# Down products as seven of quadrants, and weight sums made by transfers in memory, in a two-layer block kernel

## The chip, the cores and the metric

The kernel runs on one core of a Trainium2 chip. A core has a matrix engine (TensorE, PE in the profile; its weight loads are shown apart as PEld), a vector engine (VectorE, DVE), a scalar engine (ScalarE, ACT), GpSimd (POOL), and SyncE (SP), which here only issues transfers. Each engine works through its own queue in order and waits on semaphores of the others. Transfers run on 16 DMA engines that all queues share. The metric is the time of one execution on the device in microseconds (us), as the median of several runs.

## The reference

Two layers over 512 tokens of width 1024, all in f32. Layer 0 mixes tokens by a gated unit with a causal matrix per chunk of 128, layer 1 by forgetting attention with 12 heads; both add 4 heads of attention over 256 memory rows. After each mixing comes a gated feed-forward of hidden width 2816, which is what the change touches:

```
h = h + rmsnorm(mixed @ w_out[layer], ln_mix_post[layer])
f = rmsnorm(h, ln_ffn_pre[layer])
f = (silu(f @ w_ffn_gate[layer]) * (f @ w_ffn_up[layer])) @ w_ffn_down[layer]
h = h + rmsnorm(f, ln_ffn_post[layer])
```

## The kernel before

Every f32 number goes into TensorE as a pair of parts, hi (rounded) and lo (the rest), and a product is three matmuls, hi x hi, hi x lo and lo x hi (`mm3`, lines 182 to 184). ScalarE makes hi by a cast and VectorE lo by a subtraction (`split`, lines 239 and 240); eight buffers each of 128 x 512 hold split weights (`pair_of_parts`). A weight piece is loaded as a raw tile of 128 x 1024 (512 KB) by SP into one of four buffers.

The hidden width is 22 tiles of 128. Tiles 0 and 1 of gate and up are computed plainly while the mixing of the layer before ends (`boundary`), and their down product gives the first value of `ys`, the eight accumulators of 128 tokens x 512 outputs. The other 20 tiles go in pairs. For a pair of tiles, gate and up are each an instance of `Seven` (from line 999): the 256 rows of output, 512 tokens and 1024 inputs are cut into quadrants, and seven products of quadrants take the place of eight. `combined` makes the seven forms of the inputs once per layer. The forms of the weights need four sums, made on VectorE from two raw tiles (`sums`, lines 1022 to 1027, s3, a21 + a22, and two more), and each of the seven forms is split. `run` does one product (12 matmuls of 256 columns into a PSUM tile a, e or x) and ScalarE copies what is to be kept; `end` has VectorE add up the two halves (lines 1060, 1061, 1063) and hands them to `gate_rows` or `up_rows`, which scale, apply silu or multiply, and split the product into `fs`. `sevens` (line 1066) orders the seven products: 1, 7, 2, 6, 4, 3, 5.

`feed_forward` (line 1089) has the pairs in groups of 6, 6, 4 and 4 tiles. After each group but the last come its down products: for each half of the outputs, four PSUM tiles of 128 x 512 take 3 matmuls of 512 columns for each tile of hidden width, and VectorE adds each to `ys` (line 1174). `down_weights` loads two tiles of hidden width for one half of the outputs and splits two pieces. The last group's down products are part of `tail_of`, which also finishes the norm and, in the boundary that follows, the turn back to rows of features.

The order on each engine is set when the program is built, by a scheduler that plans the instructions with costs of its own; `behind` and `issue_after` hold an instruction back behind a named one. `last_sum` names the two sums after which the down weights may be split. A tile's buffer is given again when all its readers are done, so a load of SP waits for the split (lines 239 and 240) that read the buffer last.

## Time and profile before

| what | us |
|---|---|
| runs, median (lowest to highest) | 1113.89 (1113.71 to 1114.05) |
| profiled execution, span from first to last instruction | 1111.4 |
| TensorE busy | 1100.8 (99%) |
| VectorE busy | 893.7 (80%) |
| ScalarE busy | 660.5 (59%) |
| GpSimd busy | 25.3 (2%) |
| loads, q1 | 116.18 MB, 33.4% of 16 engines |

The profile shows one execution; its span is 2.5 us shorter than the median of the runs, which is what lies around the first and last instruction. Busy times are shares of that span. Matmuls overlap, so a record of 0.39 us can follow the one before by 0.23; the same holds to a smaller degree on VectorE and ScalarE, so costs are taken from starts, not from records. The feed-forward of layer 0 runs from about 192 to 515 us, that of layer 1 from about 778 to the end. The wait printed in square brackets is the idle time of the engine before the instruction and what ended it.

### The profile page before, as it was taken

The page shows a single profiled execution, that of the slowest core. Times are in us where ns is not written, and L with a number is a line of the kernel's source. Part 1 is how long each engine was busy: PE and PEld are TensorE (multiplying, and loading weights), DVE is VectorE, ACT ScalarE, POOL GpSimd, SP SyncE. Part 2 cuts the span into 40 slices and gives each one's busy share as a digit, 9 for nine tenths or more (in the row PEclk, how much of TensorE's full clock was granted, in tenths as well). Part 3 has the DMA queues.
Part 4 walks back from the last instruction along what each step waited for, and adds up shares of the span by engine and source line. Part 5 has one row for each costly group of instructions (what it writes and reads, how often), then busy time and mean ns, then how long its engine had stood idle before and what let it go on. Part 6 is the DMA issues. An engine that isn't in the chain of part 4 may idle for free.

```text
span 1111.4 us, 19500 instructions
## 1 busy us (share of the span) xinstructions
PE 1100.8 (99%) x7382; PEld 1000.1 (90%) x7382; DVE 893.7 (80%) x1735; ACT 660.5 (59%) x1397; POOL 25.3 (2%) x42
## 2 busy tenths in 40 slices
PE   9999999999999999999999999999999999999997
PEld 7998889998899898998988898889999899899996
DVE  8889658997697597896987898858997697687875
ACT  8776468664365264577665667668665265254553
POOL 0100000000000000001000000000000000000000
PEclk9999999999999999999999999999999999999999
DMA  7522322334133323343322654422224133333222
GB/s 267 162 76 77 98 74 76 115 109 141 57 112 97 117 92 114 97 148 117 104 88 62 173 132 116 131 76 74 79 90 154 62 114 96 101 109 114 77 76 76
DMA packets 64421, 118.12 MB, mean 106 GB/s; under 512 B 5260, under 2 KB 40088, under 8 KB 64328
## 3 DMA queue, kind: packets, MB, share of 16 engines
q1 hardware_dynamic: 63720, 116.18, 33.4%
q8 instruction: 58, 0.95, 0.4%
q0 software_dynamic: 192, 0.52, 0.2%
q14 instruction: 35, 0.29, 0.1%
q10 hardware_dynamic: 416, 0.18, 0.1%
HBM read 104.71 MB, written 2.10 MB: 96 GB/s over the span
## 4 chain that ended last, share of the span: by engine, by line
PE 94%; ACT 3%; DVE 1%; issue 1%; POOL 0%; DMA 0%; POOLq 0%; DVEq 0%; ACTq 0%
PE y L182 10%; PE y L183 10%; PE y L184 10%; PE a L182 5%; PE a L184 5%; PE a L183 5%; PE x L184 3%; PE e L182 3%; PE e L184 3%; PE e L183 3%; PE x L183 3%; PE x L182 3%; PE ps L184 3%; PE ps L183 3%; PE ps L182 3%; PE v L182 2%
## 5 line engine op out<-in xcount | busy, mean ns | idle before, releaser
L239 ACT CAST whi<-raw 128x512 fp32r<-128x512 f32 x460 | 273.1, 620 | 217.7 <-PE y L184 89.1
L240 DVE TENSOR_TENSOR wlo<-raw,whi 128x512 fp32r<-128x512 f32 x460 | 303.5, 684 | 69.5 <-ACT whi L239 67.8
L182 PE MATMUL y<-whi,fhi 128*128 128x512 f32 (+1 forms) x356 | 140.2, 394 | 0.4 <-DVE y L838 0.4
L184 PE MATMUL y<-whi,flo 128*128 128x512 f32 (+1 forms) x356 | 139.3, 391 | 0.0
L183 PE MATMUL y<-wlo,fhi 128*128 128x512 f32 (+1 forms) x356 | 139.2, 391 | 0.0
L184 PE MATMUL x<-xshi,wlo 128*128 128x256 f32 x320 | 89.9, 281 | 0.0
L182 PE MATMUL a<-xshi,whi 128*128 128x256 f32 x320 | 89.8, 281 | 0.0
L183 PE MATMUL x<-xslo,whi 128*128 128x256 f32 x320 | 89.7, 280 | 0.0
L182 PE MATMUL x<-xshi,whi 128*128 128x256 f32 x320 | 89.7, 280 | 0.0
L183 PE MATMUL a<-xslo,whi 128*128 128x256 f32 x320 | 89.7, 280 | 0.0
L184 PE MATMUL a<-xshi,wlo 128*128 128x256 f32 x320 | 89.6, 280 | 0.0
L184 PEld LDWEIGHTS y<-whi,flo 128*128 128x128 f32 x356 | 66.8, 188 | 15.7
L182 PEld LDWEIGHTS y<-whi,fhi 128*128 128x128 f32 x356 | 66.8, 188 | 15.6 <-DVE y L838 0.7
L183 PEld LDWEIGHTS y<-wlo,fhi 128*128 128x128 f32 x356 | 66.9, 188 | 14.7
L182 PEld LDWEIGHTS a<-xshi,whi 128*128 128x128 f32 x320 | 60.2, 188 | 0.5
L183 PEld LDWEIGHTS a<-xslo,whi 128*128 128x128 f32 x320 | 60.2, 188 | 0.3
L184 PEld LDWEIGHTS x<-xshi,wlo 128*128 128x128 f32 x320 | 60.3, 188 | 0.0
L183 PEld LDWEIGHTS x<-xslo,whi 128*128 128x128 f32 x320 | 60.2, 188 | 0.0
L184 PEld LDWEIGHTS a<-xshi,wlo 128*128 128x128 f32 x320 | 60.2, 188 | 0.0
L182 PEld LDWEIGHTS x<-xshi,whi 128*128 128x128 f32 x320 | 60.2, 188 | 0.0
L183 PE MATMUL ps<-xslo,whi 128*128 128x256 f32 x192 | 53.9, 283 | 0.6 <-DVE xslo L240 0.6
L184 PE MATMUL ps<-xshi,wlo 128*128 128x256 f32 x192 | 54.4, 285 | 0.0
(297 smaller groups left out, 3111.1 us busy)
## 6 DMA issues: line engine op xcount, KB each, us to landing
raw<-in_w_gate SPq DMA_DIRECT2D x44, 512.0 KB, 3.5
raw<-in_w_up SPq DMA_DIRECT2D x44, 512.0 KB, 3.6
raw<-in_w_down SPq DMA_DIRECT2D x44, 512.0 KB, 3.8
raw<-in_w_out SPq DMA_DIRECT2D x16, 512.0 KB, 4.8
raw<-in_w_b_q SPq DMA_DIRECT2D x8, 512.0 KB, 3.4
raw<-in_w_a_u SPq DMA_DIRECT2D x6, 512.0 KB
raw<-in_w_v SPq DMA_DIRECT2D x6, 512.0 KB, 4.3
raw<-in_w_k SPq DMA_DIRECT2D x6, 512.0 KB
```

The costliest lines, as they stand in the source:

```text
L182: PE.matmul(o, w[0], x[0], start=start, stop=False, skip_group_check=more)
L183: PE.matmul(o, w[0], x[1], start=False, stop=False, skip_group_check=more)
L184: return PE.matmul(o, w[1], x[0], start=False, stop=stop, skip_group_check=more)
L239: last_hi[0] = A.copy(hi, src)
L240: last_split[0] = last_hi[0], (eng or V).tensor_sub(lo, src, hi)
```

## The change

Three things go together.

1. *Down products as seven of quadrants.* Groups are now 4, 4, 4, 4 and 4 tiles. For 16 of the 22 tiles, the product of hidden rows and the down weights is cut into quadrants: 256 tokens by 256 tokens, and one half of the outputs by the other, over two tiles of hidden width. `seven_forms` makes the seven forms of the hidden values (two subtractions and two scalar operations of 256 columns, and splits of three pieces of 512 and one of 256). `Down` holds the weights of one pair of tiles, and `down_sevens` does a group's seven products for two pairs: three pairs of PSUM outputs (p, q, x), and after a product `give` adds the running sum of an output to `ys`, before the next product goes on in it. The second half of the outputs is carried with its sign turned, which the first copies and the tail undo. The down products of a group are done between the gate and the up product of the next group's first pair (`pending`), and that up's loads are ordered ahead of the block's last product (`ahead`).
2. *Two of the four weight sums of every set are made in memory.* `sums_ahead` has ScalarE issue a copy of two weight quadrants into a scratch tile in DRAM, and GpSimd a transfer that adds two others. `order_of_sums` lists them, 28 for a layer; six are made in layer 0 right after the spatial weights, and later loads each give a share of credit for one more (`load`, `credit`). A set then loads its sums, its first two quadrants and the fourth one (`a22`, on its own); two additions stay on VectorE.
3. *The order in a Seven.* 1, 7, 6, 2, 5, 4, 3; product 3 now adds to p, where 5 did last, and the x half is added right after product 2.

The core of the diff:

```diff
+    def load(dst, src):
+        last_load[0] = nc.sync.dma_start(dst, src)
+        credit[1] += credit[0]
+        while credit[1] >= 1:
+            credit[1] -= 1
+            sums_ahead()
...
+    def order_of_sums(layer):
...
+        for k0 in range(2, 22, 4):
+            to_sum.extend(gates(k0) + (downs(k0 - 4) if k0 > 2 else []) + ups(k0) + gates(k0 + 2) + ups(k0 + 2))
+
+    def sums_ahead():
+        if to_sum:
+            w, layer, m = to_sum.pop(0)
+            both = two_sums[w, layer, m] = dp.tile([P, 1040], F32, tag=name("sums"), name=name("sums"))[:, :1024]
+            with tc.issue_after(last_hi[0].ins):
+                if w == "w_down":
...
+                else:
+                    nc.scalar.dma_start(both.rearrange("p (a c) -> p a c", a=2),
+                                        i[w][layer, m : m + 2, :, :512].rearrange("a p c -> p a c"))
+                    G.dma_start(both, i[w][layer, m + 1], accum_op=ALU.add)
...
     class Seven:
-        def __init__(self, xs, src, tag, rows):
-            self.xs, self.rows = xs, rows
-            w1, w2 = loaded(src(0)), loaded(src(1))
-            self.a = [w[:, d : d + 512] for w in (w1, w2) for d in (0, 512)]
...
+        def __init__(self, xs, w, layer, m, tag, rows, late=False):
+            self.xs, self.tag, self.rows, self.late = xs, tag, rows, late
+            both = loaded(two_sums[w, layer, m])
+            raw = loaded(i[w][layer, m])
+            self.a11, self.a12 = raw[:, :512], raw[:, 512:]
+            self.s3, self.t = both[:, :512], both[:, 512:]
+            self.a22 = temp("a22")
+            nc.sync.dma_start(self.a22, i[w][layer, m + 1, :, 512:])
...
         def sums(self):
-            a11, a12, a21, a22 = self.a
-            self.s3 = temp("s3")
-            V.tensor_add(self.s3, a11, a21)
-            self.w1 = self.parts(a11)
-            V.tensor_add(a21, a21, a22)
-            self.w2 = self.parts(a12)
-            V.tensor_add(a11, a21, a11)
-            V.tensor_add(a12, a11, a12)
...
+            self.w1 = self.parts(self.a11)
+            self.w2 = self.parts(self.a12)
+            V.tensor_add(self.a11, self.t, self.a11)
+            V.tensor_add(self.a12, self.a11, self.a12)
...
-                for n in (1, 7, 2, 6, 4, 3, 5):
+                for n in (1, 7, 6, 2, 5, 4, 3):
...
+    def seven_forms(u0, u1, room):
+        left, right = (slice(*c) for c in HALVES)
+        t = temp("t3", tag="acc", bufs=2)
+        V.tensor_sub(t[:, left], u1[:, right], u0[:, right])
+        V.tensor_sub(u0[:, right], u0[:, left], u0[:, right])
+        pairs = [(act("fhi"), act("flo")) for _ in range(3)]
+        split(u0, *pairs[0])
+        split(u1, *pairs[1])
+        V.scalar_tensor_tensor(out=t[:, right], in0=u0[:, right], scalar=-1.0, in1=u1[:, right],
+                               op0=ALU.mult, op1=ALU.subtract)
+        split(t, *pairs[2])
+        V.scalar_tensor_tensor(out=u1[:, left], in0=t[:, right], scalar=-1.0, in1=u1[:, left],
+                               op0=ALU.mult, op1=ALU.subtract)
+        split(u1[:, left], *room)
...
+    def down_sevens(layer, k0, forms, ys, ahead):
+        ds = [Down(layer, k0, forms[0])]
+        ds[0].first()
+        with behind(*last_sum):
+            ds.append(Down(layer, k0 + 2, forms[1]))
+            ds[1].first()
...
+        def give(o, half, dh):
+            for t in range(2):
+                y = ys[2 * half + t][dh]
+                V.tensor_add(y, o[t], y)
...
+        for o, n in ((p, 0), (q, 1), (x, 2)):
+            product(o, n, (0,))
+        product(p, 0, (1,))
+        give(p, 0, 0)
+        product(q, 1, (1,))
+        give(q, 1, 1)
+        weights(3)
+        product(p, 3, more=True)
+        give(p, 0, 1)
+        product(x, 2, (1,))
+        give(x, 0, 0)
+        weights(6)
+        product(p, 6, more=True)
+        give(p, 1, 1)
+        weights(4)
+        product(q, 4, more=True)
+        give(q, 0, 1)
+        weights(5)
+        ahead()
+        product(p, 5, more=True)
+        give(p, 1, 0)
...
-        groups = ((2, 8), (8, 14), (14, 18), (18, 22))
+        groups = ((2, 6), (6, 10), (10, 14), (14, 18), (18, 22))
...
-            for dh in range(2):
-                outs = [ps("mm" if tb < 2 else "lg", s="y") for tb in range(TB)]
-                for kp in range(nk // 2):
-                    with behind(*(last_sum if dh + kp else ())):
-                        w = down_weights(layer, k0 + 2 * kp, dh)
-                    for x in range(2):
-                        k = 2 * kp + x
-                        for tb in range(TB):
-                            token_products(outs[tb], fs[k], w[x], tb, k == 0, k == nk - 1)
-                for tb in range(TB):
-                    V.tensor_add(ys[tb][dh], outs[tb], ys[tb][dh])
...
+            pending.append(lambda k0=k0, k1=k1, forms=forms:
+                           down_sevens(layer, k0, forms, ys, lambda: make_ahead(k1, 1)))
```

More of the change, by code (lines that the diff above doesn't have):

```diff
@@ L1112, in gate_rows, with up_rows @@
             gates[row] = g
[L1114 removed]
+        def up_rows(row, u):
             if row:
@@ L1118, in up_rows @@
                 V.tensor_mul(u, u, gates[0])
-            split(u, *fs[len(fs) - 2 + row])
+            if fs:
+                split(u, *fs[len(fs) - 2 + row])
+            elif row:
+                gates[1] = u
+            else:
+                x = len(forms)
+                forms.append(seven_forms(u, gates[1], [t[:, x, :] for t in rest]))
         fs = [(act("fhi"), act("flo")) for _ in range(2)]
@@ L1141, in feed_forward, with seven, make_ahead @@
                     token_products(o, fs[k], w[dh][k], tb, k == 0, k == 1)
-                A.copy(ys[tb][dh], o)
+                A.activation(ys[tb][dh], o, AF.Copy, scale=1.0 - 2 * dh)
+        rest = [plain("t4", (P, 2, 256), F32R) for _ in range(2)]
+        made = {}
+        def seven(m, n):
+            return Seven(xs, "w_up" if n else "w_gate", layer, m, "lg" if n else "mm", up_rows if n else gate_rows, m == 2)
+        def make_ahead(m, n):
+            u = seven(m, n)
+            made[m, n] = lambda: u
+        pending = []
+        credit[0] = 0.5 if layer else 0.3
         for gi, (k0, k1) in enumerate(groups):
-            fs = []
+            fs, forms = [], []
             for m in range(k0, k1, 2):
@@ L1148, in feed_forward @@
                     next(meanwhile)
[L1149 to L1152 removed]
+                if gi == len(groups) - 1:
+                    fs += [(act("fhi"), act("flo")) for _ in range(2)]
+                sevens(tuple(lambda n=n: made.pop((m, n), lambda: seven(m, n))() for n in range(2)), m == 2, pending)
             nk = k1 - k0
```

132 lines of the change are left out of this document (101 added, 31 removed).

## The prediction

> **What bounds the kernel now.** I read the page first, then the windows over the feed-forward of layer 0, then the timelines of TensorE and VectorE in that stretch, then the transfers.
>
> ```profile
> span 1111.4 us, 19500 instructions
> PE 1100.8 (99%) x7382; PEld 1000.1 (90%) x7382; DVE 893.7 (80%) x1735; ACT 660.5 (59%) x1397; POOL 25.3 (2%) x42
> PE 94%; ACT 3%; DVE 1%; issue 1%; POOL 0%; DMA 0%; POOLq 0%; DVEq 0%; ACTq 0%
> L182 PE MATMUL y<-whi,fhi 128*128 128x512 f32 (+1 forms) x356 | 140.2, 394 | 0.4 <-DVE y L838 0.4
> ```
>
> TensorE is busy 99% of the span, and 94% of the chain that ended last lies on it. The matmuls of the down products waited 0.4 us in all, and for the last tail. So in the feed-forward a matmul taken away is worth its whole step, as long as nobody else becomes late.
>
> ```profile
> 204.00:262.00 58.00, 58.00 (x493) 57.94 (x492) 53.13 (x95) 35.18 (x75) 0.00 (x0) 1.00 0.35 111
> 262.00:296.00 34.00, 34.00 (x152) 27.60 (x151) 21.84 (x36) 11.28 (x21) 0.00 (x0) 1.00 0.32 109
> ```
> ```profile
> ACT whi L239 <- PE y L184: 44.3, 23, 2.2
> ```
>
> The first window holds three sets of gate and up (tiles 2 to 7), the second their down products. The columns are TensorE, its weight loads, VectorE, ScalarE and GpSimd busy, the granted clock (1.00), the DMA share and GB/s. VectorE works 53.13 of 58 us in the one and 21.84 of 34 in the other: the down products are where it catches up. The last row is from the waits of ScalarE in the feed-forward of layer 0: 44.3 us go by until TensorE gives back a weight buffer, so the splits run as far ahead as their eight buffers allow.
>
> **The change, part by part.** The prices first, from the timelines of the same stretch.
>
> ```profile
> 276.73 0.39 PE L184 MATMUL y<-whi,flo 128*128 128x512 f32 x1
> 295.51 0.40 PE L184 MATMUL y<-whi,flo 128*128 128x512 f32 x1
> 231.26 0.28 PE L182 MATMUL a<-xshi,whi 128*128 128x256 f32 x1
> 238.35 0.28 PE L182 MATMUL e<-t,whi 128*128 128x256 f32 x1
> ```
> ```profile
> 262.93 0.43 DVE L1061 TENSOR_TENSOR s<-a,s 128x256 f32<-128x256 f32 x1 [2.69 <-ACT s L1049]
> 263.27 0.68 DVE L1063 TENSOR_TENSOR s<-x,s 128x512 f32<-128x512 f32 x1
> 267.48 3.69 DVE L240 TENSOR_TENSOR wlo<-raw,whi 128x512 fp32r<-128x512 f32 x6
> 275.11 0.69 DVE L1022 TENSOR_TENSOR s<-raw,raw 128x512 f32<-128x512 f32 x1 [2.88 <-DMA raw<-in_w_gate]
> 277.77 2.48 DVE L1174 TENSOR_TENSOR y<-y,y 128x512 f32<-128x512 f32 x4
> ```
>
> The first and the last of 82 matmuls of 512 columns start 18.78 us apart: 0.232 us a step. For 61 of 256 columns it is 7.09/60 = 0.118 us. On VectorE six splits take 3.69 us, five steps and one record of 0.68: 0.60 us a step; additions out of PSUM step by (2.48-0.68)/3 = 0.60 us as well. An operation of 256 columns gives way after 0.34 us (262.93 to 263.27).
>
> *Matmuls.* For every two tiles, 48 matmuls of 512 columns in down become 42. There are 16 such sets over both layers, so 96 go: 96 x 0.232 = **22.3 us off the path**. Gate and up keep their count.
>
> *VectorE, by set* (two Sevens and their share of down):
> - before: 24 operations of 512 and four of 256 in the Sevens, 4 row products, 2 splits of the rows, 4 splits and 3 additions for down: 37 x 0.60 + 4 x 0.34 = 23.6 us, beside 168 x 0.118 + 48 x 0.232 = 31.0 us of TensorE, or 76%.
> - after: 18 of 512 and 6 of 256 in the Sevens, 4 row products, the seven forms (3 splits of 512, 5 operations of 256), and for down 16 of 512 (7 splits, 2 sums, 7 evacuations): 41 x 0.60 + 11 x 0.34 = 28.3 us, beside 168 x 0.118 + 42 x 0.232 = 29.6 us, or **96%**.
>
> In a group of two sets, with one down block, VectorE then has 56.7 us of work beside 59.1 us of TensorE (61.9 before): 2.4 us of idling are free there, and the group is only slower than before once VectorE idles over 5.2 us in it. The cover for the added work is thus VectorE's old slack, and it is nearly used up. Without the two stored sums a set would have 6 additions more, 31.9 us, over TensorE's 29.6.
>
> *The down block.* Before, four PSUM outputs at a time were added to y after their last product, which nothing waited for soon. Now three pairs of outputs (p, q, x) carry seven products, and VectorE must add a running sum to y before TensorE goes on in the same output. In five of the eight blocks the built program has VectorE do the four additions of p and q ahead of the first split for product 3, and one weight sum and two additions more ahead of the second. I walk through it from the second half of product 0 on (a half is 6 matmuls, 1.39 us; a result can be read some 0.16 us after the next start, 0.39 against 0.23): the additions of p end at 2.75, of q at 4.14, the first split at 4.75, the second at 7.16, and TensorE has been idle since 6.14; then 0.4 us for the additions of product 3. The rest, 66 matmuls, want 15.3 us and end at 16.8: **1.5 us of waiting**, five times, 7.7 us. In the other three blocks both splits stand ahead of the additions, and the same walk gives none. In all eight, ScalarE's copy of product 1 of the next Seven stands right behind the cast for its second product, so hardly anything is prepared there: 0.3 us each, 2.4 us, an estimate from a cast of 0.62, the copy of 0.37, a split of 0.60 and 0.16 against one product of 1.41 us. Taken: **+10 us**. Bounds: 0, as TensorE waits for none of this today, and 8 x 2.7 = 22 us, if every block waited as long as VectorE did for a result at 262.93.
>
> *Round trips in a Seven.* Its output p is used by products 1, 6, 5, 3 with one product (1.41 us) between, where there were two.
>
> ```profile
> 306.34 0.37 ACT L1049 COPY s<-a 128x256 f32<-128x256 f32 x1
> 307.22 0.62 ACT L239 CAST whi<-raw 128x512 fp32r<-128x512 f32 x1 [0.51 <-PE a L183]
> ```
>
> 0.16 + one cast in the way 0.62 + the copy 0.37 = 1.15 us fits into 1.41, so I take 0. A second cast in the way would make 1.77, 0.4 us too late; once in each of 38 Sevens that is 14 us, the upper end.
>
> *Transfers, issues and waits.*
>
> ```profile
> q1 hardware_dynamic: 63720, 116.18, 33.4%
> raw<-in_w_gate SPq DMA_DIRECT2D x44, 512.0 KB, 3.5
> ```
> ```profile
> 0.80 0.41 ACTq L89 DMA_DIRECT2D gains<-in_gains  x1
> ```
> ```profile
> L253 POOL TENSOR_TENSOR r<-v,mhalf 128x1 f32<-128x1 f32 x16 | 9.1, 569 | 602.9 <-DVE v L845 602.9
> L382 POOL DMA_DIRECT2D memk<-memk x4 | 2.3, 572 | 312.2 <-DVE memk L380 312.2
> ```
>
> 116.18 MB took 33.4% of 16 engines' span: 3.2 us of all engines for a MB. The loads grow by 15 MB; 56 stored sums add 29 MB of copies and 29 MB of additions: some 190 MB, 55%, if an adding byte costs like a loaded one. Densest is a group in layer 1: 7.9 MB of loads and 6 sums, 6.3 MB, together 14.2 x 3.2 = 45 us of 59, or 77%. Loads then take longer than 3.5 us. A load for the second set of a down block goes out when the gate Seven before it has split its last weight; VectorE has about 8 us of other work until it needs it. 0.41 for the issue and 3.5 fit even if doubled, so I take 0; the row at 275.11, where VectorE sat 2.88 us for a load, gives the upper end, 8 x 2.9 = 23 us.
>
> The Trainium skill (Collectives: The Full Stack, section "Why ReduceScatter is half of AllGather") says that an add in a transfer is slow not by its arithmetic but because it reads two sources, which halves its rate. The trace of before has no adding transfer, so it cannot tell. By the page the sum would be that of the third rival, 1124.6 us; by the row of the loads it is 1101.6.
>
> ScalarE issues 72 copies, 72 x 0.41 = 30 us, of its 451 idle us; the casts queued behind one are covered by the buffers ahead, except next to the down blocks, whose bound covers it. Six sums, seven issues, come at once before the memory attention of layer 0 and hold its exponentials for 2.9 us; 72 value matmuls of 256 columns, 8.5 us, lie in TensorE's queue there: 0. GpSimd issues 56 additions, 56 x 0.57 = 32 us, each after its copy has landed; behind them wait only the inverse roots (569 ns), of which the first of a boundary could lose one landing, 3.5 us, at two boundaries: 0 taken, 7 the upper end. SP's loads of a sum wait for its addition; 14 sums in layer 0 and 9 in layer 1 are ordered before the first use, and three are used in a set: 0. The sign moved into the first copies of y and the subtraction in the tail replace like by like.
>
> *Sum.* 1111.4 - 22.3 + 10 = 1099.1 us of span. The median of the runs, 1113.89, lies 2.5 us over the profiled span: **1101.6 us**.
>
> **The rivals.**
> - *Nothing waits.* The walk above is too strict, the splits stay ahead: 1113.9 - 22.3 = 1091.6. For it: no wait of TensorE in before. Against it: buffers that were full at 76% cannot be filled at 96%.
> - *VectorE becomes the bound* (the slower side). Its order is fixed and it waits in it for casts, results and loads. In its fullest stretch, 204 to 262, it was busy 92% of the time. If it reaches no more, a group takes 56.7/0.916 = 61.9 us, which is just what it took before, and the 1.5 us in five blocks come on top: 1113.9 + 7.7 = 1121.6. It decides once VectorE idles over 5.2 us in a group. For it: rows like 2.69 and 2.88 above, three of them suffice. Against it: those stand where VectorE was ahead.
> - *The transfers come too late.* If an adding byte costs twice a loaded one, which no row excludes, the densest group wants (14.2 + 3.1) x 3.2 = 55 us of its 59, loads queue, and each block waits once as at 275.11: 1101.6 + 23 = 1124.6. It decides from 1.5 us a block on (12.3 us over eight). The Trainium skill's page on collectives, named above, is for this rival. Against it: 9 to 14 sums lie ahead, and 8 us of work cover a load.
> - *No change to speak of*: half of the second rival's idling, 1112 to 1116.
>
> **How the numbers follow.** My forecast (1096 to 1110) 0.42; nothing waits 0.15; VectorE bounds 0.28; late transfers 0.10; no change 0.05. Within 0.2%, 2.2 us, this kernel's runs cannot tell a change from none. Faster is 0.42 + 0.15 = 0.57, same 0.05, slower 0.38. The range leaves out the ends of the first and third rival: 1090 to 1126. The forecast alone would have 1094 to 1110.
>
> **What would show it.** Right: 1855 matmuls of 512 columns; TensorE idle only in the down blocks, before L1222's additions, 10 us together; VectorE 950 to 970 us busy (16 sets with 4.7 us more, four without a block with some 3 us less); DMA share of 50 to 65%. Wrong: TensorE waiting for splits inside the Sevens (second rival), VectorE or ScalarE waiting for loads of the stored sums (third), or GpSimd's roots late at the boundaries.

## The result, and the profile after

The changed kernel takes 1119.3 us (median of four runs, 1117.8 to 1120.4), the kernel before on the same chip 1114.0: a ratio of 1.0047, with a 95% interval of 1.0032 to 1.0061. The change makes the kernel slower by half a per cent, where 1101.6 us and a gain of 1.1% had been forecast. The profiled execution took 1117.8 us.

From the page of the changed kernel: span, busy times, DMA queues (packets, MB, share of the 16 engines), memory traffic, and the chain that ended last.

```profile
span 1116.1 us, 19812 instructions
PE 1091.6 (98%) x7286; PEld 984.6 (88%) x7286; DVE 957.5 (86%) x1895; ACT 703.0 (63%) x1513; POOL 78.7 (7%) x98
...
q1 hardware_dynamic: 71784, 130.86, 36.7%
q0 software_dynamic: 14400, 29.89, 16.4%
q10 hardware_dynamic: 28192, 29.55, 8.8%
...
HBM read 178.11 MB, written 60.82 MB: 214 GB/s over the span
...
PE 74%; DVE 12%; ACT 4%; DMA 4%; issue 3%; SPq 1%; POOL 1%; POOLq 0%; DVEq 0%; ACTq 0%
```

The 96 matmuls are gone (7382 to 7286) and TensorE has 9.2 us less to do, but its share of the chain fell from 94% to 74%. VectorE is as busy as forecast (957.5 us). The queue q0 holds the adding transfers, q10 the copies; for nearly the same bytes the first takes nearly twice the engines' time.

Where the time went shows when the span is cut at the same products in both traces: the start of the first output products of layer 0 (`y<-whi,mixedhi`), of the Sevens of both layers, of the forgetting attention (`cs`), of layer 1's output products, and of what follows each feed-forward. The four windows between these cuts that changed are shown, first of the kernel before, then of the changed one (columns: window, length, busy time of TensorE, its weight loads, VectorE, ScalarE, GpSimd; granted clock, DMA share, GB/s).

```profile
0.00:115.90 115.90, 114.19 (x734) 101.06 (x735) 97.95 (x219) 84.21 (x176) 5.95 (x12) 1.00 0.43 144
202.70:490.30 287.60, 287.60 (x2066) 270.46 (x2065) 233.89 (x403) 149.46 (x302) 0.00 (x0) 1.00 0.32 104
605.40:724.80 119.40, 119.35 (x760) 101.55 (x759) 99.94 (x231) 81.52 (x201) 0.00 (x0) 1.00 0.51 132
788.90:1077.20 288.30, 288.30 (x2074) 271.14 (x2072) 230.31 (x394) 146.14 (x294) 0.00 (x0) 1.00 0.32 103
```
```profile
0.00:119.20 119.20, 115.10 (x735) 100.94 (x735) 97.55 (x219) 83.32 (x176) 15.81 (x22) 1.00 0.80 224
206.00:489.60 283.60, 280.65 (x2017) 261.99 (x2016) 266.88 (x483) 172.05 (x361) 13.37 (x14) 1.00 0.66 184
605.10:733.80 128.70, 121.82 (x759) 102.91 (x758) 100.20 (x230) 80.63 (x201) 5.89 (x8) 0.99 0.66 164
798.00:1082.20 284.20, 282.06 (x2026) 262.90 (x2026) 263.41 (x473) 167.89 (x353) 17.48 (x18) 1.00 0.71 194
```

The two feed-forwards gained 4.0 and 4.1 us, 8.1 of the 22.3 that the matmuls are worth. Layer A lost 3.3 us and the forgetting attention 9.3. These two stretches have the same computing instructions as before, some of them in another order; what is new in them are transfers and their issues. -8.1 + 12.6 = +4.5, against +4.7 between the spans.

In layer A, this is ScalarE's timeline ahead of the first exponentials of the memory attention: seven issues (one row counts two) from 50.02 to 56.47, and, last, an issue of the feed-forward for comparison.

```profile
50.02 0.67 ACTq L175 DMA_DIRECT2D sums<-in_w_gate  x1
...
52.04 0.82 ACTq L175 DMA_DIRECT2D sums<-in_w_up  x1
52.88 1.42 ACTq L175 DMA_DIRECT2D sums<-in_w_gate  x1
54.34 2.13 ACTq L171 DMA_DIRECT2D sums<-in_w_down  x2
56.53 0.48 ACT L472 ACTIVATE mp<-mlg,nmx 128x256 f32<-128x256 f32 x1 [5.74 <-DMA sums<-in_w_up]
...
206.23 0.56 ACTq L175 DMA_DIRECT2D sums<-in_w_gate  x1
```

In the forgetting attention, the start of the first head: windows of the changed kernel, then one of the kernel before at the same work.

```profile
612.00:615.00 3.00, 2.65 (x23) 2.45 (x21) 0.48 (x1) 0.00 (x0) 0.00 (x0) 1.00 0.99 245
...
614.60:618.00 3.40, 0.17 (x2) 0.15 (x1) 0.00 (x0) 0.00 (x0) 0.00 (x0) 1.00 0.81 222
618.00:619.00 1.00, 1.00 (x4) 0.71 (x5) 0.12 (x1) 0.81 (x2) 0.00 (x0) 0.65 0.13 45
619.00:620.00 1.00, 1.00 (x5) 0.69 (x5) 0.81 (x2) 1.00 (x1) 0.00 (x0) 0.50 0.04 8
620.00:621.00 1.00, 1.00 (x7) 0.91 (x6) 0.92 (x3) 0.99 (x4) 0.00 (x0) 0.50 0.54 123
621.00:622.00 1.00, 1.00 (x8) 1.00 (x8) 0.96 (x4) 1.00 (x5) 0.00 (x0) 0.65 0.00 0
622.00:623.00 1.00, 1.00 (x12) 1.00 (x10) 0.81 (x2) 0.41 (x1) 0.00 (x0) 1.00 0.00 0
```
```profile
615.00:620.00 5.00, 5.00 (x43) 4.71 (x42) 4.57 (x12) 4.20 (x11) 0.00 (x0) 1.00 0.40 93
```

The DMA engines are full (0.99), TensorE works for 0.17 of 3.4 us, and then runs at a granted clock of 0.50 to 0.65 for four more. What it waits for are the copies of the head's queries and keys from one place of SBUF to another, directly (the second row, 5.6 of the 9.3 us) or behind ScalarE, whose cast waits for such a copy to give its buffer back. From the waits in the attention of the changed kernel, then of the kernel before, where TensorE has no wait for a copy there:

```profile
ACT whi L280 <- DMA qa<-whi: 8.5, 1, 8.5
...
PE lg L536 <- DMA ka<-whi: 5.6, 2, 3.2
```
```profile
ACT whi L239 <- DMA qa<-whi: 4.5, 1, 4.5
```

### The profile page after: what moved, and what is told of

Its sections match the earlier page's. It is cut to its first block, busy times and chain, and to the rows that moved or that the text cites. A ratio compares the mean times of both kernels' runs of the same rounds, so it can differ in the third digit from the quotient of the medians.

```text
span 1116.1 us, 19812 instructions
## 1 busy us (share of the span) xinstructions
PE 1091.6 (98%) x7286; PEld 984.6 (88%) x7286; DVE 957.5 (86%) x1895; ACT 703.0 (63%) x1513; POOL 78.7 (7%) x98
## 3 DMA queue, kind: packets, MB, share of 16 engines
q0 software_dynamic: 14400, 29.89, 16.4%
HBM read 178.11 MB, written 60.82 MB: 214 GB/s over the span
## 4 chain that ended last, share of the span: by engine, by line
PE 74%; DVE 12%; ACT 4%; DMA 4%; issue 3%; SPq 1%; POOL 1%; POOLq 0%; DVEq 0%; ACTq 0%
PE a L223 5%; PE a L225 5%; PE a L224 5%; PE y L223 4%; PE y L224 4%; PE y L225 4%; DVE wlo L281 4%; PE e L225 3%; PE e L223 3%; PE e L224 3%; PE ps L225 2%; PE ps L224 2%; PE ps L223 2%; PE p L223 2%; PE p L225 2%
## 5 line engine op out<-in xcount | busy, mean ns | idle before, releaser
L223 PE MATMUL a<-xshi,whi 128*128 128x256 f32 x464 | 131.5, 284 | 0.1
L224 PE MATMUL a<-xslo,whi 128*128 128x256 f32 x464 | 130.2, 281 | 0.0
L225 PE MATMUL a<-xshi,wlo 128*128 128x256 f32 x464 | 129.9, 280 | 0.0
L223 PE MATMUL ps<-xshi,whi 128*128 128x256 f32 x192 | 53.7, 287 | 0.0
L224 PE MATMUL p<-wlo,fhi 128*128 128x512 f32 x128 | 51.0, 399 | 1.6 <-DVE wlo L281 1.6
L223 PE MATMUL y<-whi,mixedhi 128*128 128x512 f32 x128 | 51.6, 403 | 0.0
L225 PE MATMUL p<-whi,flo 128*128 128x512 f32 x128 | 50.5, 395 | 0.0
L224 PE MATMUL y<-wlo,mixedhi 128*128 128x512 f32 x128 | 50.5, 395 | 0.0
L225 PE MATMUL y<-whi,mixedlo 128*128 128x512 f32 x128 | 50.4, 394 | 0.0
L223 PE MATMUL p<-whi,fhi 128*128 128x512 f32 x128 | 49.1, 403 | 0.7
L223 PE MATMUL a<-d2hi,whi 128*128 128x256 f32 x160 | 45.7, 285 | 1.8 <-ACT s L1085 1.7
```

Of the source, the lines that this page charges most:

```text
L223: PE.matmul(o, w[0], x[0], start=start, stop=False, skip_group_check=more)
L224: PE.matmul(o, w[0], x[1], start=False, stop=False, skip_group_check=more)
L225: return PE.matmul(o, w[1], x[0], start=False, stop=stop, skip_group_check=more)
```

## The experiments

All times below are medians, and each ratio is to runs of the kernel before on the same chip, which took 1113.5 to 1114.0 us; the ratios are those on record, and those of x11 and x14 lie 0.1% from the quotient of the two medians. The stages are the four windows above, cut in the same way in each kernel's trace: up to the first output products of layer 0 (A), feed-forward of layer 0 (F0), forgetting attention (B), feed-forward of layer 1 (F1). They come from the one profiled execution of each kernel (1117.8 us for the changed one, 1112.3 for x6, 1106.2 for x14), so they need not add up to the differences of the medians.

| kernel | us | ratio to before (95%) | A | F0 | B | F1 |
|---|---|---|---|---|---|---|
| before | 1113.8 | | 115.9 | 287.6 | 119.4 | 288.3 |
| changed | 1119.3 | 1.0047 (1.0032 to 1.0061) | 119.2 | 283.6 | 128.7 | 284.2 |
| x1 no transfers | 1094.5 | 0.9826 (0.9812 to 0.9839) | 115.8 | 277.9 | 119.9 | 277.9 |
| x8 before, with transfers | 1144.0 | 1.0270 (1.0256 to 1.0284) | 119.3 | 289.8 | 131.8 | 300.7 |
| x2 none in layer B | 1123.1 | 1.0082 (1.0051 to 1.0113) | 118.9 | 294.1 | 119.5 | 288.6 |
| x3 spread in layer A | 1125.2 | 1.0101 (1.0081 to 1.0121) | 117.0 | 290.5 | 129.9 | 285.7 |
| x4 less for VectorE | 1119.1 | 1.0055 (1.0040 to 1.0070) | 119.4 | 279.5 | 131.3 | 287.0 |
| x5 down block's order | 1119.9 | 1.0057 (1.0044 to 1.0070) | 120.0 | 283.2 | 129.4 | 285.2 |
| x6 copies alone | 1110.4 | 0.9968 (0.9956 to 0.9981) | 119.3 | 281.7 | 125.2 | 283.5 |
| x7 copy for addition | 1110.9 | 0.9977 (0.9967 to 0.9987) | 119.4 | 281.8 | 123.7 | 283.4 |
| x9 a sixteenth of the bytes | 1107.1 | 0.9939 (0.9927 to 0.9952) | 118.7 | 281.9 | 119.8 | 283.5 |
| x13 as x9, other blocks | 1105.5 | 0.9928 (0.9916 to 0.9941) | 119.3 | 281.4 | 119.4 | 284.2 |
| x16 as x9, less for VectorE | 1102.0 | 0.9899 (0.9883 to 0.9916) | 119.0 | 279.6 | 119.8 | 281.1 |
| x10 copies issued by SyncE | 1232.5 | 1.1067 (1.1052 to 1.1082) | 177.8 | 278.2 | 119.8 | 277.9 |
| x11 sums in SBUF | 1101.3 | 0.9898 (0.9883 to 0.9913) | 120.7 | 278.7 | 119.7 | 278.9 |
| x12 the same, 4 buffers | 1174.3 | 1.0527 (1.0496 to 1.0558) | 117.1 | 316.8 | 120.0 | 321.5 |
| x14 the same, 5 other buffers | 1103.7 | 0.9898 (0.9876 to 0.9919) | 120.7 | 282.7 | 119.8 | 281.0 |
| x15 as x11, roots first | 1096.8 | 0.9852 (0.9838 to 0.9867) | 117.0 | 279.1 | 119.5 | 279.0 |

### The transfers as a whole

x1 leaves all 128 transfers out; x8 puts them into the kernel before, at the same places, for nobody's use.

```
x1:  -            both = loaded(two_sums[w, layer, m])
     +            both = loaded(i[w][layer, m + 1])
     -            load(both, two_sums["w_down", layer, k])
     +            load(four(both), some(1))
     (and the list of sums to make is empty)
x8:  the kernel before + sums_ahead(), load() and the credits of the changed one
```

> The changed kernel with none of the 56 sums made: the 72 copies and 56 adding transfers are left out, and where a stored sum was loaded a tile of the plain weight of the same size is loaded instead, so the loads and all work of the engines stay and only the weights' values are not the right ones. Theory T (the transfers cost the 12.6 us that the changed kernel lost outside the feed-forward, 3.3 in layer A and 9.3 in the forgetting attention; the 15 us of stalls in the feed-forward are VectorE's): 1119.3 - 12.6 = 1106.7 us, 1104 to 1109, with the forgetting attention back at some 119.5 us and the two stretches of Sevens still at 284 to 288 us. Rival V (all of it is VectorE's load and the new order; transfers are hidden as the prediction had it): 1117 to 1120. Rival C (the transfers also make the loads and issues late inside the feed-forward): below 1100, with stretches of Sevens of 277 to 280 us.

Measured 1094.5 us: rival C. Without transfers the change gains 19.3 us, close to the rival "nothing waits" of the prediction (1091.6 us). Two windows of x1, F0 and F1:

```profile
202.70:480.60 277.90, 277.90 (x2018) 262.43 (x2017) 267.67 (x483) 172.52 (x361) 0.00 (x0) 1.00 0.43 135
780.10:1058.00 277.90, 277.90 (x2026) 262.76 (x2024) 264.44 (x474) 169.07 (x353) 0.00 (x0) 1.00 0.42 129
```

VectorE is busy for 267.67 of 277.90 us, the 96% of the prediction, and TensorE never stops. So neither VectorE's load nor the round trips cost anything by themselves. The same matmuls kept TensorE busy for 280.65 us in the changed kernel: its records stretch when it is held up, so what is lost is read from the lengths of the windows and not from its idle time.

> The kernel before with all 56 sums made at the places where the changed kernel makes them, and not used. It prices the transfers alone, with no new order in the feed-forward and VectorE at 76% there. Theory T: layer A loses some 3.4 us and the forgetting attention 8.8, as in the changed kernel, and the feed-forward, with its slack, little: 1113.8 + 12 = 1126 us, 1123 to 1132. Rival V (transfers are harmless where VectorE has slack and nobody waits for the sums): 1113 to 1117.

Measured 1144.0: the transfers with their issues, and the few instructions that the scheduler moved for them, cost the kernel before 30.4 us, more than twice what was expected, although VectorE has slack there and no load waits for a sum. A loses 3.4 us as theory T had it, B 12.4 where 8.8 were expected, F0 2.2, and F1 another 12.4. In F1 the weights come late: VectorE waits 6.3 and 5.1 us for a load of gate weights, and right behind each of these waits TensorE stands still, 6.3 and 3.2 us, for VectorE's addition to `y`. In the kernel before, VectorE's longest such wait in F1 is 3.0 us and TensorE has none. So the mechanism of the prediction's third rival does exist, but in the kernel before, at the places like the row at 275.11 from which it was priced. Landing times from 800 to 1080 us and from 605 to 730 us, of the kernel before and of x8 (KB each, median us from issue to landing):

```profile
raw<-in_w_down SPq DMA_DIRECT2D x20, 512.0 KB, 4.1
...
ka<-whi SPq DMA_DIRECT2D x24, 128.0 KB, 2.3
```
```profile
raw<-in_w_down SPq DMA_DIRECT2D x16, 512.0 KB, 7.6
...
ka<-whi SPq DMA_DIRECT2D x24, 128.0 KB, 3.8
```

What shares the DMA engines with them mostly lands later, by 1.5 us for a key copy and 3.5 for a load; not every small copy does (`qc<-whi` took 2.2 us in the attention of x8 and 2.8 before).

### Moving them elsewhere

```
x2:  -        close();  credit[0] = 0.5              (layer B)
     +        close();  credit[0] = 0                (layer 1's list is begun with layer 0's)
     -        credit[0] = 0.5 if layer else 0.3      (feed-forward)
     +        credit[0] = 0.5 if layer else 0.45
x3:  -            for _ in range(6): sums_ahead()    (layer A)
     +            credit[0] = 1                      (feed-forward 0: 0.35 for 0.3)
```

> No sum is made in layer B; the nine of them are made in the feed-forward of layer 0 instead (0.45 sums a load in place of 0.3). Theory T: the forgetting attention gets its 9.3 us back, 1119.3 - 9.3 = 1110.0 us, 1108 to 1113, the upper end if the denser feed-forward of layer 0 pays some of it. Rival V: 1118 to 1120, the forgetting attention still at 129 us. Rival C: the loss only moves into the feed-forward of layer 0: 1115 to 1119 with that stretch over 287 us.

> The six sums that were issued at one time ahead of the memory attention of layer 0 are issued one for a load from there on (and 0.35 instead of 0.3 a load in the feed-forward of layer 0). Theory T, for layer A: seven issues in a row on ScalarE hold its first exponentials for 6.5 us; without them the first output products of layer 0 start at 116 instead of 119.2 us and the time is 1119.3 - 3.3 = 1116 us, 1115 to 1118. Rival: it is the traffic and not the issues that costs there, and it stays: 1118.5 to 1120.

Both halves of theory T came out for their stage and not for the whole. x2 has the forgetting attention back at 119.5 us, but F0, now at a DMA share of 0.79, went from 283.6 to 294.1, and F1 became 4.4 slower too. In x3 layer A is 2.2 of its 3.3 us faster, and F0, with fewer sums ahead, 6.9 slower. A transfer taken from one stage collides in the next, and the waits show with what: ScalarE's casts wait 11.1 us (x2) and 11.7 us (x3) in F0 for loads of weights, against 6.9 in the changed kernel, and TensorE is idle for 8.3 and 7.4 us instead of 2.5. Why F1 became slower too in x2, where it makes fewer sums (15 additions for 18), was not tested; ScalarE waits there for loads for 14.2 us, against 3.4.

### VectorE and the order of the down block

```
x4:  -            V.tensor_add(self.a11, self.t, self.a11)        (Seven; in Down likewise)
     -            V.tensor_add(self.a12, self.a11, self.a12)
x5:  weights(3) ahead of product(q, 1, (1,)); product(x, 2, (1,)) ahead of product(p, 3);
     weights(6) ahead of give(x, 0, 0)
```

> The additions of two weight sums on VectorE are left out in every Seven and every set of down products with quadrants (12 operations of 512 columns in a group of two sets), so their products use other weights than they should; all else stays. VectorE has 56.7 - 7.2 = 49.5 us of work a group beside 59.1 of TensorE, 84%. Theory T with VectorE as the cause of the 15 us of stalls in the feed-forward: most of them go, 1119.3 - 10 = 1109 us, 1105 to 1112, both stretches of Sevens at 278 to 281 us, the losses outside unchanged. Rival (the stalls come from the order of the down blocks or from late loads): 1117 to 1120.

> Only the order in which a down block is written changes: the weights of product 3 are asked for right behind the additions of the first output, the second halves of products 1 and 2 stand ahead of product 3, and the weights of product 6 stand ahead of the additions of product 2. Theory O (the five down blocks of 20.7 to 20.8 us wait 1.2 to 1.3 us each, because VectorE adds two outputs to y before the first split of product 3, and the three of 19.5 do not): all eight at 19.5 to 19.8 us and 1119.3 - 6 = 1113 us, 1111.5 to 1115. Rival (the waits in these blocks come from late loads, transfers being in the way, and only fall into other places): blocks still over 20.5 us and 1117 to 1121.

x4 is not faster than the changed kernel: F0 gains 4.1 us, as theory T had it, and F1 and the attention lose 5.4; in F1 ScalarE now waits 26.0 us for loads, against 3.4 in the changed kernel. x5 is no faster either. Five of the eight down blocks of the changed kernel do take 20.7 to 20.8 us and three 19.5, as many as the prediction counted, and they are the five in which VectorE has four additions ahead of the first split; VectorE's timeline in the first of them, and in x1's first block:

```profile
263.03 1.29 DVE L1222 TENSOR_TENSOR y<-p,y 128x512 f32<-128x512 f32 x2 [0.53 <-PE p L225]
264.24 1.33 DVE L1222 TENSOR_TENSOR y<-q,y 128x512 f32<-128x512 f32 x2
265.49 0.68 DVE L281 TENSOR_TENSOR wlo<-raw,whi 128x512 fp32r<-128x512 f32 x1
266.09 0.68 DVE L1192 TENSOR_TENSOR raw<-raw,raw 128x512 f32<-128x512 f32 x1
266.69 1.28 DVE L1222 TENSOR_TENSOR y<-x,y 128x512 f32<-128x512 f32 x2
```
```profile
258.96 1.39 DVE L1222 TENSOR_TENSOR y<-q,y 128x512 f32<-128x512 f32 x2
260.27 0.68 DVE L281 TENSOR_TENSOR wlo<-raw,whi 128x512 fp32r<-128x512 f32 x1
261.06 0.69 DVE L1222 TENSOR_TENSOR y<-p,y 128x512 f32<-128x512 f32 x1
```

In x1 the weight sum is already made and only one split is left when the additions are done; all eight blocks have this order and take 19.5 us. But in x5, where the splits come earlier, part of the waits stays in these blocks (20.0 to 20.5 us) and the rest turns up in the Sevens. The order shows where VectorE's lateness comes out, not why it is late.

### Which of the transfers

```
x6:  both G.dma_start(..., accum_op=ALU.add) left out
x7:  -            G.dma_start(both, i[w][layer, m + 1], accum_op=ALU.add)
     +            G.dma_start(both, i[w][layer, m + 1])                    (w_down likewise)
```

In both, TensorE, VectorE and ScalarE keep every instruction in its place.

> The changed kernel without the adding transfers: the copies into the scratch stay and their rows are loaded, so the products use weights that are not sums. TensorE, VectorE and ScalarE keep their instructions in exactly the same order; 56 transfers of GpSimd, 29.89 MB and 16.4% of the DMA engines' time, are gone, and a stored row is ready one landing earlier. Theory T (what is lost beside the 6.3 us of the down blocks, 18.5 us against the kernel without any transfer, is the DMA engines' time that the transfers take): 8.8 of 25.2 parts of it stay, 1119.3 - 12 = 1107 us, 1104 to 1110. Rival I (the issues on ScalarE and the copies are what costs): 1115 to 1120.

> The adding transfers become plain copies of the same rows from the same queue (the second term is left out of the addition, so the stored rows are not sums); the engines' instructions keep exactly their order. It prices the addition itself: by its two reads the adding queue took 0.55% of the engines for a MB, a copy 0.30. Theory T: its share falls from 16.4 to about 8.8%, a third of the transfers' time, and with it a third of 18.5 us: 1119.3 - 6 = 1113 us, 1110 to 1116. Rival (the addition costs nothing that counts; the number of transfers and their waits do): 1117 to 1120.5.

The same 29.89 MB as plain copies, from the page of x7:

```profile
q0 software_dynamic: 8256, 29.89, 8.8%
```

With the addition 16.4% and 14400 packets, without it 8.8% and 8256. That alone is 8.4 us (1119.3 to 1110.9), most of it in the attention. The second copy itself costs nothing measurable (x6 and x7 differ by 0.6 us), so theory T, which gave every share of the engines the same price, was wrong on the proportion: what the addition takes more than a copy hurts most. Why is not shown; the share of the engines alone does not order these runs, as the attention took 123.7 us at a share of 0.61 in x7 and 125.2 at 0.53 in x6.

### Bytes or issues

```
x9:  all 72 copies and 56 additions on partitions 0 to 7 only ([:8]), loads as in x1
x13: x9, and no sum is started between the begin and the end of down_sevens
x16: x9, with the edit of x4
x10: -   nc.scalar.dma_start(both / four ...)     +   nc.sync.dma_start(...)
```

> The changed kernel with its 72 copies and 56 adding transfers cut to 8 of 128 partitions, a sixteenth of the bytes, and not used: the loads take plain weights of the same size instead, so the products use other weights and no load waits for an addition. TensorE, VectorE and ScalarE keep their instructions in exactly the order of the changed kernel, with the 72 issues on ScalarE. Against the kernel without any transfer (1094.5 us) it keeps the issues and the order and loses the bytes. Theory I (of the 15.9 us that are left with copies alone, the issues on ScalarE and the order that the program gets with them are the cause): 1109 us, 1106 to 1111. Theory T (the copies' bytes are): 1096 us, 1094 to 1100.

Measured 1107.1, theory I, at the lower end of its range: with the bytes gone and the 72 issues kept in the same program order, 12.6 us remain against x1. F0 and the attention of x9:

```profile
205.50:487.40 281.90, 280.00 (x2018) 261.94 (x2017) 266.95 (x483) 171.85 (x361) 11.74 (x14) 1.00 0.44 136
602.80:722.60 119.80, 119.53 (x760) 101.69 (x759) 99.68 (x230) 81.09 (x201) 4.88 (x7) 1.00 0.52 134
```

The attention is back (119.8), layer A still loses 2.9 us and the two feed-forwards 4.0 and 5.6. Its eight down blocks take the same times as those of the changed kernel to 0.02 us, so the bytes have no part in the 6.3 us that are lost there. Of the 24.8 us between x1 and the changed kernel 12.6 are thus the issues (ScalarE's 72, with GpSimd's 56 beside them) with the order that comes with them, 3.3 (1110.4 - 1107.1) the copies' bytes and 8.9 (1119.3 - 1110.4) the adding transfers. The runs of x6 lie between 1107.6 and 1112.3, so the cut between the last two is good to some 2 us only.

> The kernel with all copies and additions cut to a sixteenth of their bytes and not used, with one change: no sum is started while a down block is set up, the loads after it start it. The issues stay on ScalarE; but VectorE now has the first split for product 3 ahead of the fifth addition in all eight blocks, as in the kernel without any transfer. Theory O (of the 12.6 us between 1107.1 and 1094.5 some 6 lie in five blocks of 20.7 us, for VectorE's order there, and some 3.5 more in the Sevens around them): eight blocks of 19.5 us and 1101 us, 1098 to 1103. Theory I (it is the issues themselves, wherever ScalarE makes them): 1106 to 1108.5.

All eight down blocks put the first split early, seven take 19.4 to 19.6 us and one 19.9, and the kernel gains at most 1.6 us (1105.5, just under the range of theory I). The intervals of the two ratios overlap, and F0 and F1 together take 565.6 us as against 565.4 in x9: the Sevens take over the waiting. Theory O fell.

> Copies and additions at a sixteenth of their bytes and not used, and VectorE's additions of two weight sums left out as well (the products use other weights). Theory S (an issue on ScalarE costs because VectorE, at 96%, cannot make up for the cast that comes later): with VectorE at 84% the feed-forward loses little, both stretches of Sevens at 278 to 280.5 us; what is left of 12.6 us is the 2.9 of layer A: 1094.5 + 2.9 + 2 = 1099 us, 1097 to 1101. Theory I (an issue delays TensorE whatever VectorE does): 1105 to 1108. TensorE, VectorE and ScalarE stand in exactly the order of the earlier kernel without these additions (1119.1 us), so the difference to that one is the price of the bytes where VectorE has slack.

Measured 1102.0, between the two. With VectorE at 86% of F0, the issues cost 1.7 and 3.2 us there instead of 4.0 and 5.6. So half of their price in the feed-forward hangs on VectorE's load, as theory S has it; that VectorE fails to catch up after a late cast is its reading of this, and no run looks at single casts. The other half was not separated from the order (five blocks of 20.2 us in this build). The bytes are worth 17.1 us here (1119.1 to 1102.0).

> The copies are issued by SyncE's queue instead of ScalarE's; all bytes, additions and uses stay. TensorE then has its instructions in the same order as in the kernel without any transfer, VectorE and ScalarE but for a few (8 and 6 lines of difference), and all eight down blocks put the first split ahead of the addition of the second output. Theory I (issues and order cost 15.9 us, the additions' bytes 8.4): 1094.5 + 8.4 = 1103 us, 1100 to 1106, faster than the kernel before. Theory T (the bytes cost what is lost, whoever issues them): 1116 to 1121.

Neither theory: 1232.5. On SyncE's queue the copies went out much earlier: the sums of both layers were all started between 18 and 296 us. Layer A lost 62 us of the 138 against x1, and the stretch between it and F0 76. The first window is layer A, the second the feed-forward of layer 0.

```profile
0.00:177.00 177.00, 119.68 (x727) 104.81 (x728) 96.53 (x217) 83.85 (x176) 34.53 (x42) 0.83 1.04 266
340.00:618.00 278.00, 278.00 (x2015) 262.38 (x2014) 267.49 (x484) 172.25 (x361) 0.00 (x0) 1.00 0.43 135
```

On the issues it says nothing, since the start of the transfers moved as well; on the transfers it is clear. Where all transfers run, TensorE works 120 of 177 us; where the sums lie ready and none runs, the stages are x1's.

### The sums in SBUF

```
x11: -            both = loaded(two_sums[w, layer, m])
     +            both = raw_tile()
     +            load(<both as two quadrants>, i[w][layer, m : m + 2, :, :512])
     +            G.dma_start(both, i[w][layer, m + 1], accum_op=ALU.add)
     (Down likewise; 5 raw buffers for 4, 35 of activations for 36)
x12: 4 raw buffers and 36   x14: 5 raw, 36, and 5 of 6 results ("p")
x15: x11, and GpSimd's masking of the spatial weights behind the memory's roots
```

> No scratch and no copies: the first two quadrants are loaded into the tile in SBUF where the stored sums would have gone, and an adding transfer of GpSimd's queue adds the other two to it there. Five buffers of raw weights instead of four, 35 of activations instead of 36. The 29.55 MB of copies and the 72 issues are gone; the 56 additions lie in the feed-forward alone, where each stands between a load and its use. Theory I and theory T both have layer A and the forgetting attention back at 116 and 119.9 us. If a tile is loaded, added to (7 us) and used within the 24.6 us that five buffers give it: 1097 us, 1094 to 1102, faster than both. Rival (the additions come too late, 38 Sevens and 16 sets wait for them): above 1115.

Measured 1101.3, 1.0% faster than before: no copies, no issues on ScalarE, and the 56 additions in the feed-forwards alone, where they cost 0.8 and 1.0 us against x1. Layer A lost 4.9.

> The sums in SBUF again, with the buffers of the changed kernel: four of raw weights and 36 of activations. TensorE, VectorE and ScalarE stand in the order of the kernel without any transfer (0, 4 and 4 lines of difference); the first kernel with the sums in SBUF was built in another order in layer A, where it lost 4.9 us. If that was the order that came with 35 buffers of activations: the output products of layer 0 start at 116 us again, and with two stretches of Sevens of 278 to 279 us the time is 1101.3 - 4.9 = 1096.4 us, 1095 to 1099. Rival: four buffers give a tile 19.7 us for its load, its addition (6 to 7 us) and its use, and the Sevens wait for the additions: stretches of over 285 us, 1105 to 1120.

> The sums in SBUF with five buffers of raw weights; their room comes from one of six buffers of the Sevens' and the attention's results instead of one of activations, and the engines stand in the order of the kernel without any transfer (0, 6 and 6 lines of difference). 1096 us, 1094 to 1099, if the 4.9 us in layer A came with the order that 35 buffers of activations gave; 1101 to 1104 if the fifth buffer or the additions cost them.

x12 is the rival, in its mechanism and far beyond its range: 1174.3, with 39 and 44 us more than x1 in the feed-forwards, so a load and an addition do not fit into the turn of four buffers. x14, in x1's program order, keeps the loss in layer A, which is therefore not the order of the computing engines; it scattered more (1097.9 to 1106.2). The waits of x11 from 33 to 122 us:

```profile
POOL wsf L724 <- ACT q L396: 4.6, 1, 4.6
...
PEld rb L291 <- POOL r L294: 3.4, 1, 3.4
```

GpSimd masks the spatial weights (`wsf`) before it takes the roots of the memory's norm (`r`), and TensorE waits for the roots. x14 has the same two waits, 4.7 and 3.6 us.

> The first kernel with the sums in SBUF, with one change: GpSimd masks the spatial weights of layer A behind the inverse roots of the memory rather than ahead of them. With the fifth buffer of raw weights that masking had moved ahead, where it waited 4.7 us for its own load, and TensorE waited 3.6 us for the roots behind it. Theory: the 4.9 us in layer A are this, its output products start at 116 us again, 1101.3 - 4.9 = 1096.4 us, 1095 to 1099. Rival (the loads of a fifth buffer cost them): 1100 to 1103.

Measured 1096.8 us, ratio 0.9852 (0.9838 to 0.9867): faster than both kernels. Layer A is at 117.0, so most of the 4.9 us was that; 1.2 us of it stayed unexplained, and it is not the fifth buffer, as x12 with four has layer A at 117.1. Its page:

```profile
span 1095.0 us, 19943 instructions
PE 1083.9 (99%) x7286; PEld 984.2 (90%) x7286; DVE 959.6 (88%) x1895; ACT 705.4 (64%) x1513; POOL 80.5 (7%) x98
...
q0 software_dynamic: 14400, 29.89, 16.3%
...
PE 91%; ACT 3%; DVE 3%; issue 2%; DMA 1%; POOL 1%; SPq 0%; POOLq 0%; DVEq 0%; ACTq 0%
```

The adding transfers still take 16.3% of the engines, yet each feed-forward is only 1.1 to 1.2 us longer than in x1. Here they add into SBUF, run in the feed-forwards alone and have no copies beside them; which of the three makes them cheap was not separated.

## Why the prediction was wrong

- *Matmuls, 22.3 us.* Right in the main: x1, with nothing in the way, gains 9.7 and 10.4 us in the feed-forwards and 19.3 in all. The 2.2 us that the feed-forwards lack were not traced.
- *VectorE at 96%.* The load was right (96.3% in x1), and so was the argument that it does not bind by itself: at 96% TensorE stood still for nothing. Missing was what it means for anything else that comes late. In the changed kernel VectorE reached 94% of F0 and 93% of F1, near the 92% on which the second rival was built, and lowering its load (x16 against x9) gave 5.1 us. The rival's time (1121.6) came closer than the forecast, but that is in part luck: without the transfers and their issues its mechanism does nothing, and with them most of the bytes' price lies in the attention, where it has no part.
- *The down block, +10.* The walk counted the right five blocks and nearly their wait (1.5 forecast, 1.2 to 1.3 measured, 6 us together); the 0.3 in each of the others was not there. But x5 and x13 show that these waits are not a price of their own: with the order mended they moved into the Sevens. The feed-forwards lost 14.2 of the 22.3 us, not 10.
- *ScalarE's 72 issues, taken as 0.* This step failed. An issue took 0.62 us in the mean, not 0.41: 0.56 in most, 0.62 to 1.42 in layer A. "The casts queued behind one are covered by the buffers ahead" did not hold: with the order that came with them the issues cost 9.6 us in the feed-forwards of x9, and still 4.9 with VectorE at 86% (x16). Whether it would hold at the 76% at which those buffers were seen to be full, no run shows. The seven issues ahead of the memory attention were to take 2.9 us behind 8.5 us of value products; they took 6.5, and 2.9 us remained of it at the output products (x9).
- *Transfers, taken as 0 on the path.* This step failed, and it decided the sign: with the bytes all but gone (x9) the kernel takes 1107.1 us, inside the range of the forecast, and with them 1119.3. The share was forecast at 55% and came to 62%, since an adding byte does cost about twice a loaded one: 0.55% of the engines for a MB, loads 0.28, copies 0.30. Here the Trainium skill (Collectives: The Full Stack, section "Why ReduceScatter is half of AllGather") names the halved rate, for the adding step of a collective, and x7 agrees with it: the same bytes without the addition take 8.8 instead of 16.4%. The second read that the page gives as the reason is not shown here; the profile counts 178.11 MB read from memory with the addition and without. The prediction had this rule as its third rival, but for the changed kernel at the wrong place: there ScalarE waits for loads in the feed-forwards hardly longer than in x1 (6.9 and 3.4 us against 6.4 and 1.5). It looked for late loads ahead of the down blocks and did not ask what else uses the DMA engines while the sums are made in advance. The forgetting attention copies eight pieces of queries, keys and gates from SBUF to SBUF for each of its 12 heads, and a head's logits wait for them. There the bytes cost 9 us.
- *GpSimd's roots, 0 to 7 us; SyncE's loads of sums, 0.* The roots cost nothing in the changed kernel. They did in x11, by another piece of work on the same queue. No load waited for a sum: in the changed kernel each addition is issued at least 27 us before the load of its sum, and it has landed within 12 us.

The direction was wrong because the hidden work was priced against engines, and only in the stage that was changed. What the change is worth without its transfers, 19.3 us, was more than paid back by them: 24.8 us, 12.2 of them for bytes and 12.6 for issues and order. Left open: how these 12.6 us divide between the issues and the order the program is built in, beyond the 2.9 in layer A (the waits of the down blocks are no answer, since they moved when these were mended); and why the bytes cost 17.1 us in the build of x4 and 12.2 in the changed kernel. By the windows the difference lies in F1, where x4's loads come late, and in the attention.

## What to carry to other kernels

Work that is "made well ahead" runs in somebody else's stage: before calling a transfer hidden, list what that stage itself sends through the DMA engines, above all small copies with an engine waiting behind them, and price the transfer by their landing times. An engine that is brought to 96% can be free, as in x1, but it has little left to make up for delays: the issues on the queue that feeds it were no longer covered here. Where a sum is needed once, adding into the tile that would be loaded anyway (x15) needs one buffer more and no copy at all.

## What the runs showed of the hardware that had not been expected

- After TensorE had stood still for 3.2 us in the attention, its granted clock was down to 0.50 to 0.65 for four windows of 1 us, so that a wait costs more than its length (4 matmuls in the first of these windows, 12 in the one behind them). In x1, where it hardly waits there, the clock stays at 1.00. The Trainium skill (TensorE: Matmul & The Clock Gate, section "What's actually happening") says that the clock is either full or half, switched by the activity in windows of some 3.4 us. The trace agrees: two windows at 0.50, and two at 0.65 in which it changes.
- A transfer issue on ScalarE costs as much with a sixteenth of the bytes: in x9 the first five in layer A took 0.64 to 1.26 us each, those in the feed-forward 0.65 to 0.67, against 0.62 to 1.42 and 0.56 in the changed kernel. So its price did not fall with the size.
- An adding transfer of 512 KB landed 7.1 to 8.0 us after its issue (medians by weight, over the whole run), a plain copy of the same rows by the same queue (x7) after 4.3 to 5.3.
